# Block 2's products by token with 512 columns instead of 256, in banks that the resting attention leaves

## The chip, the cores and the metric

The kernel runs as one program on one core of a Trainium2 chip. The metric is the time of one execution on the device in microseconds (us), taken as the median over runs. Engine names as in the profile: PE is TensorE (matrix products), PEld its weight loads, DVE VectorE, ACT ScalarE, POOL GpSimd, SP SyncE (which issues DMAs).

## The reference

Two blocks over 512 tokens of width 1024, each with two layers. The change touches the second:

```python
def second_block(x, mem, ...):
    for l in range(DEPTH):                                  # 2 layers
        z = _rmsnorm(x, norm_g[l]) @ w_in[l]
        (nsa_q, nsa_kv, nsa_gate, nsa_silu, fox_qkv, fox_f, fox_silu,
         mem_q, mem_silu, merge_g) = _split(z, IN_SPLITS)
        o_a = _nsa(nsa_q, nsa_kv, ...) * silu(nsa_silu)      # 8 heads of 64, 2 key groups
        o_b = _fox(fox_qkv, fox_f, ...) * silu(fox_silu)     # 8 heads of 64, causal
        mem_kv = _rmsnorm(mem, mem_norm_g[l]) @ w_mem_kv[l]  # 256 memory rows
        o_m = _memory_xattn(mem_q, mem_kv, ...) * silu(mem_silu)   # 4 heads of 128
        g = sigmoid(merge_g).reshape(B, T, 3, D)
        u = (g[:, :, 0] * (o_a @ w_branch_a[l]) + g[:, :, 1] * (o_b @ w_branch_b[l])
             + g[:, :, 2] * (o_m @ w_branch_m[l]))
        x = x + u @ w_out[l]
```

Each attention takes a root-mean-square norm of every query and key head first; `_nsa` rotates its heads too (rope) and is the sum of three gated attentions (over compressed keys, selected blocks, a window).

## The kernel before, in words

**Arithmetic.** Every f32 operand is split into a high and a low part (`xh`, `xl` for activations, `wh`, `wl` for weights), and each product is three matmuls: high by high, high by low, low by high. A weight tile `st` comes by DMA; ACT copies `wh` out of it, and DVE (sometimes POOL) subtracts to get `wl`. In the rows below `pg<-wh,xh` is a matmul that writes bank `pg`, streams `wh` and holds `xh` as stationary weights.

**Two forms of product.** Where heads are needed token by token, `g_tm` holds 128 tokens of x and streams weights, 256 columns to a matmul; two token tiles share a bank, so the 512 tokens take two banks and 512 output columns take two passes. Where features are needed, the weights are held and 512 tokens are streamed (`pg<-xh,wh`): the merge gates (`g0`, `g1`, `g2`), the silu gates (`z0` to `z2`) and the branch outputs (`out`, `pg<-oh,wh`).

**PSUM.** Eight banks: two `pa` (scores), two `pt` (transposes), one `po` (attention values), three `pg` (products).

**Order of work.** One layer of block 2 goes through memory keys and values, memory queries, memory attention, NSA inputs, NSA attention, FoX inputs, FoX attention, the last branch's output and `w_out`. This is the foreground. The gates and branch outputs are pushed to a list of background work. Each foreground generator yields a cost, and `run` draws `cost * RATIO[i]` worth of background steps behind each yield (`pull`), the ratios standing in a table of seven:

```python
RATIO = [0.357, 0.101, 0.485, 1.137, 0.284, 0.392, 0.28]
self.pull(next(w) * r)
Fx = self.run(self.g_fox_inputs(l, pool, kp, fg), RATIO[5])
self.run(self.g_fox_attention(l, pool, Fx, zd[1], o), RATIO[6])
```

A background matmul may be put ahead of foreground work up to a distance set by `LAG`. Before `g_tm` yields `0.64 * ntok` for two slices of 128 rows of the weights, that is 20.5 us of cost for 512 columns over 512 tokens. Where a foreground waits, the background matmuls behind it fill TensorE; once the list is empty there is nothing to fill with. Four of `g1`'s tiles are held back to the end of FoX attention (`HELD`).

Of the kernel before, what the change touches and what calls it, by code (L numbers as in the profile page):

```python
# [19 lines left out]
T = 512  # L20
D = 1024
# [85 lines left out]
class Net:  # L107
# [507 lines left out]
    def rope_table(self, pool, tag, cs, g, a):  # L615

        c = self.t(pool, [128, NT, 64], tag + "c", bufs=1)
        s = self.t(pool, [128, NT, 64], tag + "s", bufs=1)
# [10 lines left out]
    def rope(self, pool, dst, src, tab, b, a):  # L629

        c, s = tab
        nh = src.shape[2]
        x, y = (
            self.t(pool, [128, 128 * nh], n).rearrange("p (t h d) -> p t h d", t=2, h=nh)
            for n in ("rpx", "rpy")
        )
        self.tt(x, src, bch(c[:, 2 * b : 2 * b + 2, :], nh, 2), ALU.mult)
        for j in range(2):
            si = src[:, j].rearrange("p h (a t f) -> p h a t f", a=a, t=2)
            yo = y[:, j].rearrange("p h (a t f) -> p h a t f", a=a, t=2)  # L640
            sj = s[:, 2 * b + j, :].rearrange("p (a t f) -> p a t f", a=a, t=2)
# [5 lines left out]
        self.tt(dst, x, y, ALU.add, self.G)  # L647

    def head_ms(self, pool, ms, src, b, h0, tag="hsq", bufs=None):

        _, _, nh, d = src.shape
        sq = self.t(pool, [128, T], tag, bufs=bufs)[:, 0 : 2 * nh * d].rearrange("p (t h d) -> p t h d", t=2, h=nh)
        self.act(sq, src, AF.Square)
        for j in range(2):
            self.V.tensor_reduce(ms[:, 2 * b + j, h0 : h0 + nh], sq[:, j], AX.X, ALU.add)
# [17 lines left out]
    def bank(self, g):  # L673

        return self.t(self.pa, [128, T], "pa") if g else self.t(self.pt, [128, T], "pt")

# [720 lines left out]
    def g_mem_inputs(self, l, pool):  # L1397
# [32 lines left out]
        def evac_k(b, ps):  # L1430
            k = ps.rearrange("p t (h d) -> p t h d", d=128)
            self.head_ms(ip, ks, k, 0, 2 * len(kr))
            a = self.t(ip, [128, D], "mt")[:, 0:T].rearrange("p (t h d) -> p t h d", t=2, h=2)
            self.act(a, k)
            kr.append(a)

        for c in range(2):
            yield from self.g_tm(w, D, 256 * c, mh, ml, evac_k, 2)
# [3 lines left out]
        for c in range(2):  # L1442
            for t in range(2):
                self.tt(kr[c][:, t], kr[c][:, t], bc(rk[:, t, 2 * c : 2 * c + 2], 128), ALU.mult)
            for i in range(2):
                kh, kl = self.t(pool, [128, T], "kh", F32R, bufs=4), self.t(pool, [128, T], "kl", F32R, bufs=4)
                self.to_fm(kh[:, 0:256], kl[:, 0:256], [kr[c][:, t, i] for t in range(2)])
                K.append((kh, kl))
        vv = []
        for c in range(2):  # L1450
            v = self.t(pool, [128, 2, 2, 256], "v", F32R)
            vh, vl = v[:, 0], v[:, 1]

            def evac_v(b, ps, vh=vh, vl=vl):
                for t in range(2):
                    self.split(vh[:, t], vl[:, t], ps[:, t], rm[:, t : t + 1])

            yield from self.g_tm(w, D, 512 + 256 * c, mh, ml, evac_v, 2)
            vv.append((vh, vl))
# [3 lines left out]
    def g_mem_query(self, l, pool):  # L1463
# [5 lines left out]
        for c in range(2):  # L1469
            qb = self.t(ip, [128, NT, 2, 128], "qb")  # L1470
            ms, r = (self.small(8, n, 2).rearrange("p (t h) -> p t h", t=NT) for n in ("qms", "qr"))

            def evac(b, ps, ms=ms, qb=qb):
                q = ps.rearrange("p t (h d) -> p t h d", d=128)
                self.head_ms(ip, ms, q, b, 0)
                for j in range(2):
                    self.tt(qb[:, 2 * b + j], q[:, j], bch(g, 2, 1), ALU.mult)

            yield from self.g_tm(I["w_in_2"][l], D, 3872 + 256 * c, self.xh, self.xl, evac)
            self.head_r(r, ms, 128, 128**-0.5, self.rt, self.rt2)  # L1480
            self.scale_heads(qb, r)
            for i in range(2):
                qh, ql = self.t(pool, [128, T], "qh", F32R, bufs=4), self.t(pool, [128, T], "ql", F32R, bufs=4)
                self.to_fm(qh, ql, [qb[:, t, i] for t in range(NT)])
                Q.append((qh, ql))
# [98 lines left out]
    def g_nsa_inputs(self, l, pool, fg):  # L1584
# [6 lines left out]
        tks = [  # L1591
            self.rope_table(rp, f"tk{b}", cs, self.row(rp, "nsa_k_norm_2", l, 64, b + 1, f"gk{b}"), 1) for b in range(2)
        ]
        kc, vc = yield from self.g_nsa_compress(l, pool, cs)
        ip, cm = self.pool(f"ni{l}", bufs=2)
        Q = []
        for c in range(2):
            qb = self.t(ip, [128, NT, 4, 64], "qb")
            msq, rq = (self.small(16, n, 2).rearrange("p (t h) -> p t h", t=NT) for n in ("msq", "rq"))

            def evac_q(b, ps, msq=msq, qb=qb):
                q = ps.rearrange("p t (h d) -> p t h d", d=64)
                self.head_ms(ip, msq, q, b, 0)
                self.rope(ip, qb[:, 2 * b : 2 * b + 2], q, tq, b, 1)

            yield from self.g_tm(w, D, 256 * c, self.xh, self.xl, evac_q)
            self.head_r(rq, msq, 64, 0.125, self.rt, self.rt2)
            self.scale_heads(qb, rq)
            for i in range(2):
                a = self.t(pool, [128, T], "qh", F32R, bufs=4), self.t(pool, [128, T], "ql", F32R, bufs=4)  # L1610
                self.to_heads(a, [qb[:, t, 2 * i : 2 * i + 2, :].rearrange("p h d -> p (h d)") for t in range(NT)])
                Q.append(a)
        K, vv = [], []
        for br in range(2):
            tk = tks[br]
            msk = self.small(8, "msk", 2).rearrange("p (t h) -> p t h", t=NT)
            rk = self.small(8, "rk", 2).rearrange("p (t h) -> p t h", t=NT)
            v = self.v_tiles(pool, 2)
            kr = []

            def evac_k(b, ps, v=v, kr=kr, msk=msk, tk=tk):
                k = ps[:, :, 0:128].rearrange("p t (h d) -> p t h d", d=64)
                self.head_ms(ip, msk, k, b, 0)
                kb = self.t(ip, [128, 2, 2, 64], "kb")
                self.rope(ip, kb, k, tk, b, 1)
                kr.append(kb)
                for j in range(2):
                    self.split_v(v, 2 * b + j, ps[:, j, 128:256])

            yield from self.g_tm(w, D, 768 + 256 * br, self.xh, self.xl, evac_k)  # L1630
            self.head_r(rk, msk, 64, 1.0, self.rt, self.rt2)
            kd = self.t(ip, [128, NT, 2, 2, 64], "qb")
            for t in range(NT):
                for u in range(2):
                    self.tt(kd[:, t, :, u, :], kr[t // 2][:, t % 2], bc(rk[:, t, :], 64), ALU.mult, self.G)
# [6 lines left out]
            vv.append(v)  # L1642
# [71 lines left out]
    def g_fox_inputs(self, l, pool, kp, fg):  # L1714
# [22 lines left out]
        Q, K, vv = [], [], []  # L1737
        for c in range(2):
            for kind in range(2):
                ms = self.small(16, "fms", 2).rearrange("p (t h) -> p t h", t=NT)  # L1740
                b4 = self.t(ip, [128, NT, 4, 64], "qb", bufs=3)

                def evac(b, ps, kind=kind, ms=ms, b4=b4):
                    q = ps.rearrange("p t (h d) -> p t h d", d=64)
                    self.head_ms(pool, ms, q, b, 0, "p", 3)
                    for j in range(2):
                        if kind == 0:
                            self.tt(b4[:, 2 * b + j], q[:, j], bch(g, 4, 1), ALU.mult)
                        else:
                            self.act(b4[:, 2 * b + j], q[:, j])  # L1750

                yield from self.g_tm(w, D, 1816 + 512 * kind + 256 * c, self.xh, self.xl, evac)
                r = self.small(16, "fr", 2).rearrange("p (t h) -> p t h", t=NT)
                self.head_r(r, ms, 64, 1.0, self.rt, self.rt2)
                if kind == 0:
                    self.scale_heads(b4, r)
                for i in range(2):
# [5 lines left out]
                    kd = self.t(ip, [128, NT, 2, 2, 64], "qb", bufs=3)  # L1763
# [8 lines left out]
            v = self.v_tiles(pool, 4)  # L1772

            def evac_v(b, ps, v=v):
                for j in range(2):
                    self.split_v(v, 2 * b + j, ps[:, j])

            yield from self.g_tm(w, D, 2840 + 256 * c, self.xh, self.xl, evac_v)
            vv.append(v)
# [179 lines left out]
```

## Time and profile before

| | |
|---|---|
| time, 3 runs | 3091.78, 3096.23, 3097.36 us; median 3096.23 |
| the profiled execution | 3096.09 us, of which the span is 3094.3 us |
| PE busy (modelled) | 3011.5 us, 97% |
| DVE, ACT, POOL busy | 2221.3 us (72%), 1502.0 us (49%), 416.4 us (13%) |
| layer 1 of block 2 | from 1773.1 to 2438.7 us of the span, 665.6 us |
| layer 2 of block 2 | from 2438.7 us to the end |

The ends of matmuls are modelled in the profile: a 512-column matmul is given 0.39 us, though the next starts sooner. So "busy" hides short waits of PE; what a matmul costs is read from one start to the next.

### The profile page before, as it was taken

What the parts mean: (1) busy time and instruction counts of PE and PEld (TensorE: products, weight loads), DVE (VectorE), ACT (ScalarE), POOL (GpSimd) and SP (SyncE); (2) the same over time, 40 slices, a digit from 0 to 9 for tenths busy, and PEclk for the clock granted to TensorE, in tenths of its full rate; (3) what the DMA queues carried; (4) which work ended last, traced back from release to release, by engine and by line L of the source; (5) the groups of instructions that cost most, each with busy time, mean ns of one, the idle gap of its engine ahead of it and who ended that gap; (6) DMA issues with size and microseconds to landing.
All of it is one profiled execution on the core that took longest, in us unless ns stands there. A gap on an engine that the chain in (4) does not pass through costs nothing. (4 is left out here: it accounts for less than half of the span.)

```text
span 3094.3 us, 54458 instructions
## 1 busy us (share of the span) xinstructions
PE 3011.5 (97%) x20148; PEld 2540.6 (82%) x20148; DVE 2221.3 (72%) x4974; ACT 1502.0 (49%) x3043; POOL 416.4 (13%) x550
## 2 busy tenths in 40 slices
PE   8989999999999899999999999999999999999999
PEld 6877778888888777788888898888888898878977
DVE  5988776777448887777774466778686666788684
ACT  3544744444324456544443344366464453476463
POOL 2433300000014343100000000200100010200200
PEclk9999999999999999999999999999999999999999
DMA  4435125333343342253333454522435545422525
GB/s 146 115 90 146 43 88 175 96 99 96 125 129 89 106 120 85 68 167 107 98 98 123 136 140 131 143 75 73 123 113 186 158 118 150 121 66 67 162 87 183
DMA packets 403116, 359.02 MB, mean 116 GB/s; under 512 B 32867, under 2 KB 350307, under 8 KB 402851
## 3 DMA queue, kind: packets, MB, share of 16 engines
q1 hardware_dynamic: 396707, 335.62, 37.6%
q0 software_dynamic: 6144, 19.93, 1.8%
q8 instruction: 159, 2.61, 0.4%
q14 instruction: 106, 0.87, 0.1%
HBM read 293.98 MB, written 61.47 MB: 115 GB/s over the span
## 5 line engine op out<-in xcount | busy, mean ns | idle before, releaser
L260 ACT ACTIVATE wh<-st 128x512 fp32r<-128x512 f32 x844 | 528.2, 629 | 788.5 <-PE pg L238 633.4
L254 DVE TENSOR_TENSOR wl<-st,wh 128x512 fp32r<-128x512 f32 x766 | 539.0, 705 | 402.0 <-ACT wh L260 397.2
L238 PE MATMUL pg<-xh,wh 128*128 128x512 f32 (+1 forms) x1824 | 733.0, 402 | 3.6 <-ACT wh L260 2.2
L238 PE MATMUL pg<-xh,wl 128*128 128x512 f32 (+1 forms) x1824 | 719.9, 395 | 5.3 <-POOL wl L254 5.3
L238 PE MATMUL pg<-xl,wh 128*128 128x512 f32 (+1 forms) x1824 | 712.2, 395 | 0.0
L238 PEld LDWEIGHTS pg<-xl,wh 128*128 128x128 f32 (+1 forms) x1824 | 343.4, 188 | 73.8 <-issue 0.4
L238 PEld LDWEIGHTS pg<-xh,wl 128*128 128x128 f32 (+1 forms) x1824 | 344.2, 189 | 72.0 <-POOL wl L254 7.0
L238 PEld LDWEIGHTS pg<-xh,wh 128*128 128x128 f32 (+1 forms) x1824 | 344.2, 189 | 70.7 <-ACT wh L260 2.6
L238 PE MATMUL pg<-wl,xh 128*128 128x256 f32 x928 | 265.1, 287 | 0.4 <-DVE wl L254 0.4
L238 PE MATMUL pg<-wh,xh 128*128 128x256 f32 x928 | 262.6, 287 | 1.1 <-DVE oz L257 0.8
L238 PE MATMUL pg<-wh,xl 128*128 128x256 f32 x928 | 263.0, 285 | 0.0
L238 PEld LDWEIGHTS pg<-wh,xh 128*128 128x128 f32 x928 | 176.3, 192 | 6.2 <-DVE oz L257 1.0
L238 PEld LDWEIGHTS pg<-wl,xh 128*128 128x128 f32 x928 | 177.9, 192 | 3.9 <-DVE wl L254 0.8
L238 PEld LDWEIGHTS pg<-wh,xl 128*128 128x128 f32 x928 | 177.7, 192 | 1.2
L485 POOL DMA_DIRECT2D xd<-xn x40 | 21.8, 544 | 1049.5 <-DVE xn L257 927.5
L254 POOL TENSOR_TENSOR wl<-st,wh 128x512 fp32r<-128x512 f32 x78 | 123.1, 1584 | 267.5 <-ACT wh L260 234.4
L238 PE MATMUL pg<-hh,wl 128*128 128x512 f32 x352 | 137.0, 389 | 0.0
L238 PE MATMUL pg<-hh,wh 128*128 128x512 f32 x352 | 136.7, 389 | 0.0
L238 PE MATMUL pg<-hl,wh 128*128 128x512 f32 x352 | 135.7, 389 | 0.0
L260 ACT ACTIVATE p<-pa,anb 128x128 f32<-128x128 f32 (+1 forms) x224 | 115.6, 517 | 36.9 <-DVE anb L725 34.0
L257 DVE SCALAR_TENSOR_TENSOR u<-pad,cols,u 128x512 f32<-128x512 f32 x176 | 127.3, 746 | 0.7
L260 ACT ACTIVATE ph<-pt 128x128 fp32r<-128x128 f32 (+1 forms) x224 | 94.9, 426 | 65.9 <-PE pt L251 64.5
(509 smaller groups left out, 6276.2 us busy)
## 6 DMA issues: line engine op xcount, KB each, us to landing
st<-in_w_in_dram SPq DMA_DIRECT2D x400, 256.0 KB
st<-in_w_up_dram SPq DMA_DIRECT2D x176, 256.0 KB
st<-in_w_down_dram SPq DMA_DIRECT2D x88, 256.0 KB
st<-in_w_out_dram SPq DMA_DIRECT2D x64, 256.0 KB
xo<-xd SPq DMA_DIRECT2D x48, 256.0 KB
th<-thz SPq DMA_DIRECT2D x48, 256.0 KB
xd<-xn POOLq DMA_DIRECT2D x40, 256.0 KB, 4.0
thd<-thz SPq DMA_DIRECT2D x32, 256.0 KB
```

The costliest lines, as they stand in the source:

```text
L238: return self.pe(self.PE.matmul(out, lhsT, rhs, start=start, stop=stop, **kw))
L254: return (eng or self.V).tensor_tensor(out, a, b, op)
L257: return self.V.scalar_tensor_tensor(out, a, s, b, op0, op1)
L260: return self.S.activation(out, in_, f, **kw)
L485: self.nc.gpsimd.dma_start(self.xd[:, k, :], x)
```

## The change

A new product `g_tmw` gives each tile of 128 tokens a bank of its own and streams 512 columns to a matmul. Three of the four banks are those of the attention, which rests meanwhile (`wide`: `pa, pa, po, pg`, or `pg, pa, pa, pg` for FoX queries, which start under the last NSA heads); memory keys and values, with two token tiles, take the two `pa`. It loads one slice of 128 rows by 512 columns at a time, as many loads and bytes as before. It yields `1.28 * len(ps)` for each slice: 41.0 of cost for 512 columns over 512 tokens.

It is used for memory keys, values and queries, NSA queries, the keys and values of NSA's two branches (together now), and FoX queries, keys and values. Compression in NSA and all of block 1 keep `g_tm`. The norms and rope are taken for one token tile with 8 heads instead of two tiles with 4, and head tiles are kept in the attention's buffers. FoX goes through all queries, all keys, all values, where before it did queries, keys and values of four heads and then of the other four. The tables `RATIO` and `LAG` stay as they are.

```diff
+    def g_tmw(self, w, K, c0, xh, xl, evac, banks):
+        ps = [self.t(p, [128, T], n) for p, n in banks]
+        nk = K // 128
+        for k in range(nk):
+            wh, wl = self.wload(w, k, 1, [(c0, 512)])
+            for t, o in enumerate(ps):
+                a, b = xh[k][:, 128 * t : 128 * t + 128], xl[k][:, 128 * t : 128 * t + 128]
+                self.mm(o, a, wh[:, 0], start=(k == 0), stop=False)
+                self.mm(o, a, wl[:, 0], start=False, stop=False)
+                self.mm(o, b, wh[:, 0], start=False, stop=(k == nk - 1))
+            if k + 1 < nk:
+                yield 1.28 * len(ps)
+        for t, o in enumerate(ps):
+            evac(t, o)
+        yield 1.28 * len(ps)
+
+    def wide(self, inner=True):
+        pa, pg = (self.pa, "pa"), (self.pg, "pg")
+        return (pa, pa, (self.po, "po"), pg) if inner else (pg, pa, pa, pg)
...
-            yield from self.g_tm(I["w_in_2"][l], D, 3872 + 256 * c, self.xh, self.xl, evac)
+        yield from self.g_tmw(I["w_in_2"][l], D, 3872, self.xh, self.xl, evac, self.wide())
...
-            yield from self.g_tm(w, D, 256 * c, self.xh, self.xl, evac_q)
+        yield from self.g_tmw(w, D, 0, self.xh, self.xl, evac_q, self.wide())
...
-            yield from self.g_tm(w, D, 768 + 256 * br, self.xh, self.xl, evac_k)
+        yield from self.g_tmw(w, D, 768, self.xh, self.xl, evac_k, self.wide())
...
-        for c in range(2):
-            for kind in range(2):
-                yield from self.g_tm(w, D, 1816 + 512 * kind + 256 * c, self.xh, self.xl, evac)
+        for kind in range(2):
+            yield from self.g_tmw(w, D, 1816 + 512 * kind, self.xh, self.xl, evac, self.wide(bool(kind)))
...
-            yield from self.g_tm(w, D, 2840 + 256 * c, self.xh, self.xl, evac_v)
+        yield from self.g_tmw(w, D, 2840, self.xh, self.xl, evac_v, self.wide())
```

TensorE has 15,542 rows in its order before and 14,136 after. The matmuls of the products that change number 1344 of 256 columns in each layer before, and 672 of 512 after. Counted in the order, for one layer (layer 2 has 10 of FoX's queries on the other side of the border between its fifth and sixth stage):

| stage (up to) | background gate matmuls | foreground product matmuls | branch-output matmuls |
|---|---|---|---|
| ahead of the first memory product | +12 | | |
| memory keys, values (first query product) | 36 → 57 | 181 → 96 | |
| memory queries (first score) | 39 → 120 | 203 → 96 | |
| memory attention (its last value product) | 132 → 51 | 96 → 86, compression's | |
| NSA inputs (first compressed score) | 128 → 99 | 384 → 202 | 96 → 96 |
| NSA attention (its last value product) | 259 → 261 | 118 → 52 | 0 → 5 |
| FoX, up to its last product | 6 → 90 | 458 → 236 | 78 → 91 |
| FoX attention, from there | 144 → 54 | | 20 → 9 |

Under NSA attention DVE makes 26 `wl`, 11 `tha` and 3 `thz` of gate work before, 20, 10 and 2 after, and two more `kl`.

Two places in TensorE's order. The first is the FoX inputs of layer 1, a slice of the weights in the last product, for the values. Before, two slices of 256 columns go to half a bank for one token tile after the other (`pg_24942` and `pg_24943` are the two banks):

```order
L238 MATMUL pg_24942<-wh_24981,xl_3547_17615 128x256
L238 MATMUL pg_24942<-wh_24981,xh_3540_17608 128x256
L238 MATMUL pg_24942<-wl_24982,xh_3540_17608 128x256
L238 MATMUL pg_24942<-wh_24981,xl_3548_17616 128x256
L238 MATMUL pg_24943<-wl_24982,xh_3539_17607 128x256
L238 MATMUL pg_24943<-wh_24981,xl_3547_17615 128x256
L238 MATMUL pg_24943<-wh_24981,xh_3540_17608 128x256
```

After, a slice of 512 columns goes to four banks (two `pa`, `po`, `pg_24201`), and nine gate matmuls into another `pg` follow it:

```order
L238 MATMUL pa_24198<-wh_24377,xl_3550_17618 128x512
L238 MATMUL pa_24199<-wh_24377,xh_3542_17610 128x512
L238 MATMUL pa_24199<-wl_24378,xh_3542_17610 128x512
L238 MATMUL pa_24199<-wh_24377,xl_3550_17618 128x512
L238 MATMUL po_24200<-wh_24377,xh_3542_17610 128x512
L238 MATMUL po_24200<-wl_24378,xh_3542_17610 128x512
L238 MATMUL po_24200<-wh_24377,xl_3550_17618 128x512
L238 MATMUL pg_24201<-wh_24377,xh_3542_17610 128x512
L238 MATMUL pg_24201<-wl_24378,xh_3542_17610 128x512
L238 MATMUL pg_24201<-wh_24377,xl_3550_17618 128x512
L238 MATMUL pg_24399<-xh_3537_17605,wh_24401 128x512
L238 MATMUL pg_24399<-xh_3537_17605,wl_24402 128x512
```

Gate work that stood behind FoX attention's heads now stands between the slices of its products. The second place is FoX attention of layer 1. Before, gate matmuls (`pg<-xh,wh`) stand between the scores (`pa`), values (`po`) and transposes (`pt`) of a head:

```order
L238 MATMUL pa_25411<-pch_23820,sel_130 128x128
L238 LDWEIGHTS identb_94
L238 MATMUL pa_25411<-neg_124,identb_94 128x128
L238 MATMUL pg_25553<-xh_3537_17605,wh_25555 128x512
L238 MATMUL pg_25553<-xh_3537_17605,wl_25556 128x512
L238 MATMUL pg_25553<-xl_3545_17613,wh_25555 128x512
L238 MATMUL po_25152<-pl_25211,v_24288 64x256
L238 MATMUL po_25152<-ph_25210,v_24288 128x256
L238 MATMUL po_25152<-pl_25211,v_24288 64x256
L238 MATMUL po_25152<-ph_25210,v_24288 128x256
```

After, from the first score to the two last heads, only attention is left:

```order
L238 MATMUL pa_24604<-pch_23343,sel_130 128x128
L238 LDWEIGHTS identb_94
L238 MATMUL pa_24604<-neg_124,identb_94 128x128
L238 MATMUL po_24502<-ph_24503,v_24196 128x256
L238 MATMUL po_24502<-pl_24504,v_24196 64x256
L238 MATMUL po_24502<-ph_24503,v_24196 128x128
L238 MATMUL po_24502<-pl_24504,v_24196 64x128
L238 MATMUL pa_24621<-kh_24106,ql_23700 128x256
L238 MATMUL pa_24621<-kl_24107,ql_23700 128x256
```

The gate product that stood in the first piece has moved ahead of the whole attention. In memory attention the same holds for eight of its sixteen tiles.

## Rows read from the trace of the kernel before

**Rows 1.** The page, part 1: busy us (share of the span) and instructions.

```profile
PE 3011.5 (97%) x20148; PEld 2540.6 (82%) x20148; DVE 2221.3 (72%) x4974; ACT 1502.0 (49%) x3043; POOL 416.4 (13%) x550
```

**Rows 2.** Busy time by stretch: the stages of layer 1 of block 2.

```profile
core 0: us, PE busy (x) PEld busy (x) DVE busy (x) ACT busy (x) POOL busy (x), PEclk, DMA share, GB/s
1773.10:1808.20 35.10, 32.88 (x239) 30.54 (x237) 25.41 (x71) 18.96 (x37) 0.00 (x0) 1.00 0.50 151
1808.20:1843.10 34.90, 34.90 (x254) 32.87 (x255) 22.68 (x63) 14.28 (x27) 2.78 (x4) 1.00 0.50 128
1843.10:1902.00 58.90, 58.90 (x372) 52.71 (x371) 40.10 (x111) 34.45 (x88) 10.28 (x15) 1.00 0.48 136
1902.00:2020.90 118.90, 117.66 (x748) 102.59 (x746) 80.11 (x225) 38.84 (x80) 22.52 (x32) 1.00 0.48 135
2020.90:2184.20 163.30, 158.40 (x1028) 134.17 (x1027) 135.33 (x417) 107.74 (x285) 3.27 (x4) 0.98 0.25 68
2184.20:2274.60 90.40, 90.40 (x646) 84.46 (x645) 60.13 (x140) 40.40 (x80) 16.74 (x39) 1.00 0.53 154
...
2349.00:2438.70 89.70, 89.70 (x406) 74.53 (x406) 57.39 (x100) 38.87 (x68) 4.36 (x8) 1.00 0.61 194
```

**Rows 3.** Busy time by stretch: FoX attention of layer 1, in pieces.

```profile
2264.30:2349.00 84.70, 80.78 (x487) 66.65 (x486) 68.77 (x161) 59.47 (x149) 1.59 (x5) 1.00 0.35 103
2288.90:2330.70 41.80, 38.39 (x250) 31.47 (x250) 37.35 (x95) 33.55 (x90) 0.00 (x0) 1.00 0.24 71
2323.40:2330.70 7.30, 5.95 (x40) 4.78 (x41) 6.39 (x17) 6.24 (x19) 0.00 (x0) 1.00 0.18 67
2330.70:2349.00 18.30, 18.30 (x97) 15.35 (x96) 10.68 (x21) 8.52 (x18) 0.00 (x0) 1.00 0.49 146
```

**Rows 4.** Timeline of PE in a run of 512-column matmuls: start us, us, instruction.

```profile
1692.81 0.39 PE L238 MATMUL pg<-hl,wh 128*128 128x512 f32 x1
...
1695.98 0.39 PE L238 MATMUL pg<-hh,wl 128*128 128x512 f32 x1
```

**Rows 5.** The same in a run of 256-column matmuls, the product for NSA's keys.

```profile
1999.70 0.28 PE L238 MATMUL pg<-wh,xh 128*128 128x256 f32 x1
...
2001.74 0.28 PE L238 MATMUL pg<-wh,xl 128*128 128x256 f32 x1
```

**Rows 6.** Groups of DVE instructions: busy us, mean ns, idle time before them.

```profile
L254 DVE TENSOR_TENSOR wl<-st,wh 128x512 fp32r<-128x512 f32 x762 | 536.7, 706 | 401.5 <-ACT wh L260 396.7 <-issue 0.2
L257 DVE SCALAR_TENSOR_TENSOR tha<-pg,R 128x512 f32<-128x512 f32 x112 | 77.0, 688 | 50.7 <-PE pg L238 35.6 <-ACT R L260 10.3 <-ACT thz L260 4.0
L730 DVE RECIPROCAL ari<-asm 128x1 f32<-128x1 f32 x288 | 45.1, 157 | 32.4 <-ACT p L260 30.5
L254 DVE TENSOR_TENSOR pl<-pt,ph 128x256 fp32r<-128x256 f32 x80 | 33.3, 419 | 18.5 <-ACT ph L260 18.2
L725 DVE TENSOR_REDUCE anb<-pa 128x1 f32<-128x256 f32 x80 | 32.8, 418 | 7.6 <-PE pa L238 6.7
L257 DVE SCALAR_TENSOR_TENSOR thz<-thz,tha 128x512 f32<-128x512 f32 x32 | 24.2, 755 | 1.1 <-ACT thz L260 0.7
L254 DVE TENSOR_TENSOR kl<-pt,kh 128x512 fp32r<-128x512 f32 x24 | 15.8, 682 | 5.0 <-ACT kh L260 5.0
L737 DVE TENSOR_SCALAR p<-p,ari 128x256 f32<-128x256 f32 x32 | 11.4, 358 | 0.6
```

**Rows 7.** Timeline of DVE in memory attention of layer 1, where a head ends.

```profile
1868.86 0.69 DVE L254 TENSOR_TENSOR oz<-po,thz 128x512 f32<-128x512 f32 x1 [2.25 <-PE po L238]
...
1870.80 0.68 DVE L254 TENSOR_TENSOR ol<-oz,oh 128x512 fp32r<-128x512 f32 x1
```

**Rows 8.** One tile over the whole program, NSA query rope: ns min/median/max.

```profile
L254 DVE TENSOR_TENSOR rpx<-pg,tqc x8: 669/681/693, 1955.4 to 2642.3; 128x512 f32<-128x512 f32 x8
```

**Rows 9.** Busy time by stretch at NSA's compressed scores of layer 1 (columns as in Rows 2).

```profile
2020.00:2025.00 5.00, 5.00 (x36) 4.79 (x34) 2.20 (x8) 1.46 (x4) 0.00 (x0) 0.78 0.37 97
2025.00:2030.00 5.00, 5.00 (x18) 4.27 (x18) 4.63 (x18) 1.76 (x5) 0.00 (x0) 0.53 0.01 2
```

More of the change, by code (lines that the diff above doesn't have):

```diff
@@ L1441, in g_mem_inputs @@
         K = []
[L1442 to L1448, printed above, removed]
+        for t in range(2):
+            self.tt(kr[t], kr[t], bc(rk[:, t], 128), ALU.mult)
+        for i in range(4):
+            kh, kl = self.t(pool, [128, T], "kh", F32R, bufs=4), self.t(pool, [128, T], "kl", F32R, bufs=4)
+            self.to_fm(kh[:, 0:256], kl[:, 0:256], [kr[t][:, i] for t in range(2)])
+            K.append((kh, kl))
         vv = []
@@ L1451, in g_mem_inputs, with evac_v @@
             v = self.t(pool, [128, 2, 2, 256], "v", F32R)
[L1452 to L1459, printed above, removed]
+            vv.append((v[:, 0], v[:, 1]))
+        def evac_v(t, ps):
+            for c in range(2):
+                self.split(vv[c][0][:, t], vv[c][1][:, t], ps[:, 256 * c : 256 * c + 256], rm[:, t : t + 1])
+        yield from self.g_tmw(w, D, 512, mh, ml, evac_v, pas)
         cm.__exit__(None, None, None)
@@ L1468, in g_mem_query, with evac @@
         Q = []
[L1469 to L1477, printed above, removed]
-            yield from self.g_tm(I["w_in_2"][l], D, 3872 + 256 * c, self.xh, self.xl, evac)
[L1480 to L1485, printed above, removed]
+        qb = self.t(ip, [128, NT, 4, 128], "qb", bufs=1)
+        ms, r = (self.t(ip, [128, NT, 4], n, bufs=1) for n in ("qms", "qr"))
+        def evac(t, ps):
+            q = ps.rearrange("p (t h d) -> p t h d", t=1, d=128)
+            self.head_ms(ip, ms, q, t, 0)
+            self.tt(qb[:, t], q[:, 0], bch(g, 4, 1), ALU.mult)
+        yield from self.g_tmw(I["w_in_2"][l], D, 3872, self.xh, self.xl, evac, self.wide())
+        self.head_r(r, ms, 128, 128**-0.5, self.rt, self.rt2)
+        self.scale_heads(qb, r)
+        for i in range(4):
+            qh, ql = self.t(pool, [128, T], "qh", F32R, bufs=4), self.t(pool, [128, T], "ql", F32R, bufs=4)
+            self.to_fm(qh, ql, [qb[:, t, i] for t in range(NT)])
+            Q.append((qh, ql))
         cm.__exit__(None, None, None)
@@ L1590, in g_nsa_inputs @@
         tq = self.rope_table(rp, "tq", cs, self.row(rp, "nsa_q_norm_2", l, 64), 1)
-        tks = [
-            self.rope_table(rp, f"tk{b}", cs, self.row(rp, "nsa_k_norm_2", l, 64, b + 1, f"gk{b}"), 1) for b in range(2)
-        ]
+        tkc, tks = (self.t(rp, [128, 2, NT, 64], n) for n in ("tkc", "tks"))
+        for b in range(2):
+            gk = self.row(rp, "nsa_k_norm_2", l, 64, b + 1, f"gk{b}")
+            self.rope_table(rp, None, cs, gk, 1, (tkc[:, b], tks[:, b]))
         kc, vc = yield from self.g_nsa_compress(l, pool, cs)
@@ L1596, in g_nsa_inputs @@
         Q = []
-        for c in range(2):
[L1598 to L1604, printed above, removed]
-            yield from self.g_tm(w, D, 256 * c, self.xh, self.xl, evac_q)
-            self.head_r(rq, msq, 64, 0.125, self.rt, self.rt2)
-            self.scale_heads(qb, rq)
+        x4 = self.heads4(pool, "ph"), self.heads4(pool, "ph")
@@ new lines, in g_nsa_inputs, with evac_q @@
+        msq, rq = (self.t(ip, [128, NT, 8], n, bufs=1) for n in ("msq", "rq"))
+        def evac_q(t, ps):
+            q = ps.rearrange("p (t h d) -> p t h d", t=1, d=64)
+            self.head_ms(ip, msq, q, t, 0)
+            self.rope(ip, [a[:, t : t + 1] for a in x4], q, tq, t, 1)
+        yield from self.g_tmw(w, D, 0, self.xh, self.xl, evac_q, self.wide())
+        self.head_r(rq, msq, 64, 0.125, self.rt, self.rt2)
+        for c in range(2):
+            self.scale_heads(x4[c], rq[:, :, 4 * c : 4 * c + 4])
@@ new lines, in g_nsa_inputs, with evac_k @@
+        K, vv, kr = [], [self.v_tiles(pool, 2) for _ in range(2)], []
+        msk, rks = (self.t(ip, [128, NT, 4], n, bufs=1) for n in ("msk", "rk"))
+        def evac_k(t, ps):
+            p3 = ps.rearrange("p (r x) -> p r x", r=2)
+            k = p3[:, :, 0:128].rearrange("p r (h d) -> p r h d", d=64)
+            sq = self.t(ip, [128, T], "hsq")[:, 0:256]
+            self.act(sq.rearrange("p (r h d) -> p r h d", r=2, h=2), k, AF.Square)
+            V.tensor_reduce(msk[:, t], sq.rearrange("p (h d) -> p h d", h=4), AX.X, ALU.add)
+            kb = self.t(ip, [128, 2, 2, 64], "kb", bufs=4)
+            self.rope(ip, kb, k, (tkc[:, :, t], tks[:, :, t]), 0, 1)
+            kr.append(kb)
+            for br in range(2):
+                self.split_v(vv[br], t, p3[:, br, 128:256])
```

112 lines of the change are left out of this document (54 added, 58 removed).

## The prediction

> **What bounds the kernel now.** I read the page first: TensorE is busy for 3011.5 of 3094.3 us [rows 1]. That share hides the point. The ends of matmuls are modelled, so I went to the busy time by stretch and, inside it, to the starts of matmuls. In layer 1 the stages with products have TensorE busy throughout, and DVE for a half to two thirds of the time (34.9 us with DVE 22.7, 90.4 with 60.1). The attention stages are different: in NSA attention DVE has 135.3 of 163.3 us and TensorE is no longer full [rows 2]. In FoX attention, five heads of 41.8 us have DVE at 37.4; the one head of them that has no gate work between its matmuls takes 7.3 us with DVE at 6.4 and ACT at 6.2 [rows 3]. So a product stage pays for each matmul that is put into it, while an attention head goes at the pace of DVE and ACT, and gate work there costs TensorE little but costs DVE its `wl` and `tha`.
>
> This is the frame for the change. Work on TensorE that is saved in a product stage is time saved. Gate work that is moved from an attention to a product is paid in full where it goes, and gives back only what the attention loses in length.
>
> **Issue.** In a run of 512-column matmuls, 14 starts lie 3.17 us apart, 0.226 us each [rows 4]; with 256 columns, 17 starts take 2.04 us, 0.120 us each [rows 5]. A pair of the latter replaced by one of the former saves 0.014 us. There are 672 such pairs in a layer, so 9.1 us, and 18.3 us over both layers. The lower bound for this is nothing (0.240 us for one matmul, if four banks in turn are as slow as two halves).
>
> The loads stay as they are in number and size (one slice of 512 columns for two of 256, and SP issues as many DMAs), and with the DMA engines at half their time in these stages [rows 2] I put the new order of loads at nothing.
>
> A rule speaks against the size of this gain. The Trainium skill, "TensorE: Matmul & The Clock Gate", section "Back-to-back issue gap", gives the isolated gap as N/2.4 + 2.5 ns. By that a pair of 256 columns takes 218 ns and one of 512 takes 216, and 1344 pairs save an estimated 3.4 us in place of 18.3. The rows differ from it (120 and 226 ns), and the measurement decides.
>
> **Where the background goes.** The yields of the changed products are twice what they were (41.0 against 20.5 for 512 columns) and the ratios are the same, so each product draws twice the gate work. I counted TensorE's order, stage by stage, and priced each at 0.226 us for a 512-column matmul. For one layer:
>
> Memory keys, values and queries: 102 gate matmuls more, +23.1 us; 384 matmuls of 256 columns become 192 of 512, −2.6. Together +20.5 on 70.0 us.
>
> Memory attention: 81 gate matmuls fewer, −18.3, and 10 of compression's 256-column ones leave, −1.2. But eight of its sixteen tiles are now without cover. DVE needs 0.418 + 0.157 + 0.419 us for each, 0.358 for every second one, whose scaling it shares with ACT [rows 6], and 0.69 + 0.68 us at the end of each of two heads [rows 7]: 12.1 us. TensorE has 12 matmuls of 256 columns and 4 transposes of 128 for two tiles, 1.7 us at the starts above, 6.7 for eight. The difference, 5.4 us, becomes visible. Together −14.1 on 58.9 us. The bounds of the 5.4 are 0 (DVE catches up under the tiles that keep cover) and 9 (each pair waits for its chain).
>
> NSA inputs: 29 gate matmuls fewer, −6.6; 384 matmuls of 256 become 192 of 512, −2.6; compression's 10 arrive, +1.2. The gate work now runs out before the keys' product, as it did before, but all eight query heads become ready at once and the next product wants the banks that they are read from. A copy-out of 512 columns by rope is 0.68 us on DVE for its first part [rows 8], and three or four such steps stand ahead of the second bank. I take +2, between 0 and +5. Together −6.0 on 118.9 us.
>
> NSA attention: the same background (259 and 261 matmuls), but DVE's share of it is smaller: six `wl`, one `tha` and one `thz` fewer, two `kl` more. That is 6 x 0.706 + 0.688 + 0.755 − 2 x 0.682 = 4.3 us by [rows 6]. Since DVE is busy for 83% of this stage [rows 2], I take −3.6, between −7 (TensorE's 118 query matmuls that become 52 count too) and +1.
>
> FoX inputs: 97 gate and branch matmuls come ahead of the end of its last product, +22.0; 458 of 256 columns become 236 of 512, −1.5.
>
> FoX attention: today the stretch from the end of the last product to the last head is 84.7 us, and the last two heads, which carry the held gate work in both kernels, take 18.3 of it [rows 3]. After, six heads without cover: 6 x 7.3 = 43.8 us. In front of them comes a start. Before, the first scores stand inside the last product. After, that product owns the score banks, so four banks must be copied out and a first tile must go through the chain. My estimate for it is 3.5 us, some five DVE instructions of 0.4 to 0.7 us. 3.5 + 43.8 + 18.3 = 65.6, −19.1. A head between 6.4 us, its DVE time, and 8.3, the mean of the five heads that are covered now, moves this by −5 to +6.
>
> Ahead of the block: 12 gate matmuls more, +2.7.
>
> The sum for a layer: +20.5 − 14.1 − 6.0 − 3.6 + 22.0 − 1.5 − 19.1 + 2.7 = +0.9; for both, +1.8 us. The profiled execution took 3096.1 us, the median is 3096.2, so the forecast is 3098 us. The 18.3 us that TensorE saves is all given back, because attention stages that have lost their filler don't get shorter by as much as the products have grown. The smaller number of norm instructions I put at nothing: they lie on DVE in product stages, where it is busy for 65%, so TensorE covers them; without that cover they would be worth 1 or 2 us.
>
> **Rivals.**
>
> *The attentions shrink further.* What speaks for it: a head's DVE time is 6.4 us and not 7.3, and with nothing else in DVE's and ACT's queues a head may come to that. Against it: the head of 7.3 us is such a head already, and both engines had 0.9 to 1.1 us of gaps in it [rows 3]. With 6.4 us for a head (−5.4 in a layer) and half of the memory tiles' 5.4 us, it is 8.1 us in a layer: 3082 us. With all lower bounds together, 3070.
>
> *The clock falls in the bare attention; the other side.* A head's columns are 3 x 1280 for scores, 2 x 1280 for values, 1280 for transposes and 512 for masks, 8192 in all: 16 times a 512-column matmul, 3.6 us at full clock. At half clock they are 7.2 us, as long as the whole head, so TensorE would become the bound there. At NSA's compressed scores, where TensorE ran short matmuls in a row, the granted clock was 0.78 and then 0.53, near the lower of its two levels, 1.2 GHz [rows 9]. Against it: in the head without gate work it was 1.00 [rows 3]. The price is between 0 and 3.6 us a head; with half, 1.8 x 12 heads = 22 us: 3120 us. [...] The Trainium skill, same page, section "HAM oscillation — how this bites in real kernels", tells of a kernel that cycles through PSUM banks, whose small idle times between groups make the clock swing. In this case's trace, products that take two banks in turn had 1.00 [rows 2]; four banks are not in it.
>
> *Four banks finish at once and the next product waits.* Six borders in a layer (memory keys to values, values to queries, NSA queries to keys, keys to attention, FoX queries to keys, keys to values) each copy out four banks with 8 heads; DVE takes some 2 us for one bank, three times 0.68 [rows 8]. Five of them exposed with 2 us each, of which 2 are in the sum already, are 8 us in a layer: 3114 us. Against it: where gate matmuls are left they stand between, and these borders have them except after NSA's queries.
>
> *It doesn't do what it says*: if a 512-column matmul into four banks in turn starts every 0.240 us, the gain of 18.3 us is gone and the rest stays: 3116 us.
>
> **How the numbers follow.** Chances: the sum as worked out 0.44, attentions shrink further 0.28, the clock 0.09, the borders 0.13, no gain from width 0.06. A measurement of this kernel can tell about 0.2% from no change, 6.2 us. The likeliest case has its own range from 3088 to 3108, and leaves the 6.2 us on either side in a fifth of its cases, 0.09 each. So faster is 0.28 + 0.09 = 0.37, slower 0.28 + 0.09 = 0.37, and within 0.2% is 0.26. The range from 3074 to 3122 takes in the rivals' times at both ends, short of all lower bounds together.
>
> **What would show each step.** Starts 0.226 us apart in the changed products, with `pa`, `pa`, `po`, `pg` in turn, show the first term. Memory keys, values and queries should be about 90 us, memory attention 45, NSA inputs 113, NSA attention 160, the stretch of FoX products up to the end of the last one 101 (80.1 before, 2184.2 to 2264.3 us [rows 2, 3]), the rest of FoX 66. Six FoX heads of 7.3 us without `wl` between them, at a clock of 1.00, show the largest term. The prediction is wrong if heads come at 6.4 or 8.3 us, if the clock in FoX attention is near 0.5, or if TensorE has gaps of 2 us or more at the borders of products.

## The result

The changed kernel is slower: 3112.73 us, median of 4 runs (3108.72 to 3116.27), against 3095.43 us for the kernel before in the same measurement. The ratio is 1.0057, with a 95% interval from 1.0045 to 1.0070. The forecast was 3098 us, in a range from 3074 to 3122. The profiled execution has a span of 3112.9 us, 18.6 us more than before.

The width itself came as forecast. The timeline of PE in the last FoX product of the changed kernel, twelve matmuls from row to row:

```profile
2287.46 0.39 PE L238 MATMUL pa<-wh,xh 128*128 128x512 f32 x1
...
2290.18 0.39 PE L238 MATMUL pg<-xh,wh 128*128 128x512 f32 x1
```

Twelve starts in 2.72 us are 0.227 us each, across the four banks `pa`, `pa`, `po`, `pg`: what a run of 512 columns showed [rows 4]. So four banks in turn cost nothing here.

The busy time by stretch, changed kernel, layer 1 (columns as in Rows 2). The borders are the first memory product, first query product, first score, last value product, first compressed score, last NSA value product, end of the last FoX product, last FoX value product:

```profile
core 0: us, PE busy (x) PEld busy (x) DVE busy (x) ACT busy (x) POOL busy (x), PEclk, DMA share, GB/s
1776.30:1813.50 37.20, 37.20 (x171) 30.24 (x170) 25.90 (x65) 19.49 (x37) 0.00 (x0) 1.00 0.62 176
1813.50:1863.90 50.40, 50.40 (x229) 41.62 (x228) 27.54 (x55) 18.54 (x33) 4.93 (x4) 1.00 0.47 126
1863.90:1904.20 40.30, 39.88 (x274) 36.04 (x273) 29.82 (x81) 26.30 (x74) 5.07 (x9) 1.00 0.41 116
1904.20:2012.80 108.60, 108.60 (x529) 86.90 (x527) 70.23 (x176) 37.65 (x78) 17.04 (x22) 1.00 0.51 144
2012.80:2189.60 176.80, 165.79 (x986) 135.72 (x985) 135.32 (x414) 108.65 (x287) 8.66 (x18) 0.95 0.24 68
2189.60:2290.10 100.50, 100.41 (x469) 83.08 (x468) 61.85 (x119) 40.39 (x71) 20.20 (x40) 1.00 0.53 159
2290.10:2360.30 70.20, 60.30 (x380) 48.10 (x379) 58.09 (x149) 51.96 (x141) 0.00 (x0) 1.00 0.22 65
```

By the same borders the kernel before took 33.1, 34.9, 57.5, 120.3, 163.2, 80.2 and 84.7 us. Against the forecast, us a layer:

| stage | forecast | layer 1 | layer 2 |
|---|---|---|---|
| memory keys, values, queries | +20.5 | +19.6 | +20.3 |
| memory attention | −14.1 | −17.2 | −17.2 |
| NSA inputs | −6.0 | −11.7 | −11.7 |
| NSA attention | −3.6 | +13.6 | +9.5 |
| FoX up to its last product | +20.5 | +20.3 | +19.5 |
| FoX attention | −19.1 | −14.5 | −14.3 |

The products grew as worked out. What the attentions gave back is where it failed, above all in NSA: inputs and attention together were to get 9.6 us shorter and got 1.9 longer in layer 1 and 2.2 shorter in layer 2. (The two have to be taken together. In layer 1 the transposes of the keys ended at 2020.8 us before, ahead of the first compressed score at 2020.9; now that score starts at 2012.8 and the keys' transposes only at 2023.9, so work of the inputs has moved over the border.) DVE is busy for 135.3 us in NSA attention, as before [rows 2], so the stage did not get more to do. It waits.

**Where NSA waits.** The timeline of DVE in the changed kernel, behind the compressed scores (in brackets the idle time ahead of an instruction, and what ended it):

```profile
2022.98 0.98 DVE L254 TENSOR_TENSOR wl<-st,wh 128x512 fp32r<-128x512 f32 x1 [2.04 <-ACT wh L260]
2027.67 0.19 DVE L254 TENSOR_TENSOR fx<-fg,r_fox_f_bias 128x32 f32<-128x32 f32 x1 [3.71 <-DMA r_fox_f_bias<-in_fox_f_bias_dram]
2027.78 0.68 DVE L254 TENSOR_TENSOR kl<-pt,kh 128x512 fp32r<-128x512 f32 x1
2028.38 0.17 DVE L1749 TENSOR_SCALAR fx<-fx 128x32 f32<-128x32 f32 x1
2028.46 0.69 DVE L254 TENSOR_TENSOR kl<-pt,kh 128x512 fp32r<-128x512 f32 x1
```

DVE stands for 3.7 us in front of a 32-column addition that belongs to FoX's gate, until the gate's bias has been loaded. Behind it in DVE's order stand the low halves of NSA's keys (`kl`). The timelines of SP and of POOL show when the bias is loaded:

```profile
2015.22 9.13 SPq L402 DMA_DIRECT2D st<-in_w_in_dram  x2
2024.96 0.34 SPq L386 DMA_DIRECT2D r_fox_f_bias<-in_fox_f_bias_dram  x1
```

```profile
2018.34 6.60 POOL L254 TENSOR_TENSOR pl<-kb,rk 128x128 f32<-128x128 f32 x16 [10.75 <-issue]
```

Its DMA stands behind two weight loads that hold SP for 9.1 us until a buffer is free. But what it waits for last is POOL, which scales the keys (`kb`) until 2024.94 us; 0.02 us later it is issued. In the kernel the bias has its buffer in the pool of FoX's inputs, which is opened when the pool of NSA's inputs, with `kb` in it, is closed; that the two share memory is read from this order and from the wait. The kernel with half yields (below) tells the two causes apart. There SP issues its last weight load at 2010.98 us, and the bias waits for POOL all the same, until 2018.61. SP's waits for it there and in the changed kernel, in this order (us in all, times, longest):

```profile
SPq L386 <- POOL pl L254: 6.3, 1, 6.3
SPq L386 <- POOL pl L254: 0.5, 1, 0.5
```

PE waits in turn:

```profile
2028.61 0.63 PE L251 MATMUL pt<-c_ident,pl 128*128 128x128 f32 x4 [2.15 <-DVE fx L1749]
```

Before, DVE waited 1.5 us for this load over both layers; now 7.4. The keys of both branches now become ready behind one product and are scaled in one run of 16, so the bias is loaded later, and the wait falls in front of the keys' low halves.

**Where FoX starts.** The timeline of PE, from the last matmul of the value product, and of DVE at the end of the first head:

```profile
2289.96 0.39 PE L238 MATMUL pg<-wh,xl 128*128 128x512 f32 x1
...
2291.54 0.22 PE L238 MATMUL pa<-kh,qh 128*128 128x128 f32 x1
...
2293.87 0.45 PE L238 MATMUL pa<-kh,qh 128*128 128x384 f32 x1 [1.33 <-ACT p L260]
```

```profile
2306.14 0.67 DVE L254 TENSOR_TENSOR ol<-oz,oh 64x512 fp32r<-64x512 f32 x1
...
2314.45 0.69 DVE L254 TENSOR_TENSOR ol<-oz,oh 64x512 fp32r<-64x512 f32 x1
...
2320.31 0.66 DVE L254 TENSOR_TENSOR ol<-oz,oh 64x512 fp32r<-64x512 f32 x1
```

From the end of the product to the end of the first head it takes 16.7 us, where the forecast had 10.8. The heads after it end 8.3 and 5.9 us apart in turn, five of them in 36.7 us, 7.3 each as forecast, at a clock of 1.00. The rest, with the last two heads, takes 16.8 us, where the forecast had 18.3.

### The profile page after: what moved, and what is told of

The parts are those of the page before. It is cut to its first block, busy times and chain, and to the rows that moved or that the text cites. A ratio compares the mean times of both kernels' runs of the same rounds, so it can differ in the third digit from the quotient of the medians.

```text
span 3112.9 us, 51600 instructions
## 1 busy us (share of the span) xinstructions
PE 3012.3 (97%) x18804; PEld 2473.7 (79%) x18804; DVE 2194.3 (70%) x4758; ACT 1497.9 (48%) x3035; POOL 415.4 (13%) x550
## 5 line engine op out<-in xcount | busy, mean ns | idle before, releaser
L238 PE MATMUL po<-ph,v 128*128 128x256 f32 x480 | 124.5, 287 | 8.5 <-ACT ph L260 8.0
L754 DVE TENSOR_REDUCE anb<-pa 128x1 f32<-128x128 f32 (+1 forms) x224 | 105.9, 475 | 25.7 <-PE pa L238 23.6
L254 DVE TENSOR_TENSOR pl<-pt,ph 128x128 fp32r<-128x128 f32 (+1 forms) x224 | 105.1, 473 | 23.5 <-ACT ph L260 22.4
L238 PE MATMUL po<-pl,v 128*64 128x256 f32 (+1 forms) x448 | 106.7, 279 | 7.6 <-DVE pl L254 7.5
L257 DVE SCALAR_TENSOR_TENSOR tha<-pg,R 128x512 f32<-128x512 f32 x112 | 76.7, 685 | 47.4 <-PE pg L238 32.6
L254 DVE TENSOR_TENSOR pad<-pg,R 128x512 f32<-128x512 f32 x112 | 77.4, 691 | 44.7 <-PE pg L238 35.9
```

Of the source, the lines that this page charges most:

```text
L238: return self.pe(self.PE.matmul(out, lhsT, rhs, start=start, stop=stop, **kw))
L254: return (eng or self.V).tensor_tensor(out, a, b, op)
L257: return self.V.scalar_tensor_tensor(out, a, s, b, op0, op1)
L754: self.V.tensor_reduce(nb, ps[:, 0:n], AX.X, ALU.max, negate=True)
```

## The experiments

The theory after the result: the width saves its 18 us; the doubled draw of gate work takes more than that away, by itself, in FoX, and by NSA's keys having nothing over them. The rival: the loss comes from the borrowed banks and from what the change does to the order of keys and heads, whatever is drawn. Times are medians; the ratio is to the kernel before on the same chip.

**Half yields.** Both yields of `g_tmw`:

```diff
-                yield 1.28 * len(ps)
+                yield 0.64 * len(ps)
...
-        yield 1.28 * len(ps)
+        yield 0.64 * len(ps)
```

> The changed kernel with half the yields in the wide product, so that a product draws as much gate work as before. By the order of instructions FoX gets its gate matmuls back (12 ahead of the end of the last product and 147 after it, as before), while memory keeps most of the shift (112 of 120 gate matmuls stay under the queries). Theory 1, the doubled draw empties FoX attention and that is the loss there: FoX comes back from 170.7 us a layer to about 163 (before 164.9, less 1.4 of issue), total about 3098. Theory 2, FoX loses because its first head cannot start inside the products any more: filled heads get longer again by what the products get shorter, FoX about 168, total about 3107.

3077.99 us, ratio 0.9941 (0.9926 to 0.9956): faster than both kernels, by 20 us more than theory 1 had for it. The stretches of layer 1 (the same borders):

```profile
1773.90:1804.70 30.80, 29.85 (x137) 23.95 (x137) 23.39 (x62) 17.80 (x33) 0.00 (x0) 1.00 0.60 175
1804.70:1853.40 48.70, 48.70 (x222) 40.15 (x221) 26.53 (x55) 18.55 (x33) 4.49 (x4) 1.00 0.50 132
1853.40:1897.80 44.40, 43.78 (x301) 40.05 (x300) 32.59 (x94) 28.02 (x79) 7.51 (x11) 1.00 0.45 123
1897.80:2010.40 112.60, 112.60 (x542) 90.41 (x541) 71.22 (x174) 39.72 (x79) 15.66 (x20) 1.00 0.50 141
2010.40:2172.60 162.20, 154.85 (x973) 126.73 (x972) 131.08 (x404) 107.57 (x285) 8.32 (x18) 1.00 0.25 70
2172.60:2250.10 77.50, 77.50 (x365) 64.41 (x364) 50.40 (x104) 33.34 (x59) 18.05 (x40) 1.00 0.53 159
2250.10:2336.60 86.50, 82.49 (x496) 67.91 (x495) 70.02 (x167) 60.48 (x155) 0.00 (x0) 1.00 0.35 102
```

FoX takes 164.0 us, near the 163 of theory 1. The rest of the difference to the changed kernel is in NSA (274.8 against 285.4) and memory (123.9 against 127.9). One thing didn't follow the draw: 112 gate matmuls still stand under the memory queries (120 in the changed kernel, 39 before). The first score wants a bank that the product holds, and the `z2` work that has to be done ahead of the attention is done here. So that shift belongs to the order and the banks, not to the yields (argued from the order, not tried by itself). FoX attention is 1.8 us longer than before, with the same gate work in it.

**The draw alone, in the kernel before.** `g_tm` gets a cost of 1.28 in the seven products:

```diff
-        yield 0.64 * ntok
+        yield cost * ntok
```

> The kernel before with the yields of the seven products doubled and nothing else: the redistribution without wide matmuls and without borrowed banks. By the sum of the prediction the emptied attentions cost what width saves, so about 3096 + 18 = 3114. If the loss comes from the borrowed banks and the late keys instead (theory 2), FoX inputs get 20 us longer and FoX attention 17 to 20 shorter, NSA and memory stay, and the total is 3096 to 3103.

3116.07 us, ratio 1.0065 (1.0050 to 1.0080), +20.6 us: the amount by which the prediction's sum has the width given back (18.3 + 1.8). Not by its stages, though: memory, NSA and FoX of layer 1 are the stretches

```profile
1773.60:1813.40 39.80, 39.80 (x270) 36.68 (x271) 28.96 (x77) 21.11 (x41) 0.00 (x0) 1.00 0.59 172
1813.40:1844.80 31.40, 31.40 (x239) 30.26 (x238) 16.26 (x45) 11.45 (x20) 2.77 (x4) 1.00 0.41 106
1844.80:1911.00 66.20, 65.44 (x395) 57.57 (x394) 44.75 (x126) 35.60 (x90) 10.15 (x15) 1.00 0.50 138
1911.00:2016.80 105.80, 104.98 (x691) 92.15 (x690) 75.02 (x219) 35.29 (x73) 18.24 (x25) 1.00 0.48 135
2016.80:2185.70 168.90, 164.87 (x1053) 139.11 (x1053) 137.03 (x421) 109.02 (x287) 5.82 (x11) 0.97 0.26 72
2185.70:2287.90 102.20, 102.20 (x698) 94.49 (x697) 63.43 (x141) 42.74 (x81) 18.44 (x40) 1.00 0.54 155
2287.90:2358.70 70.80, 61.61 (x372) 49.53 (x371) 56.42 (x141) 50.25 (x134) 0.00 (x0) 0.95 0.21 64
```

memory +11.9, NSA −8.8, FoX +8.1, where the changed kernel has +2.4, +1.9 and +5.8. So the doubled draw is a loss without wide products too, but that its total meets the prediction's sum is in part luck. In FoX the doubled draw without wide products gives nearly what the changed kernel has: inputs 22 us longer, attention 13.9 shorter. In its bare FoX attention the clock did fall, in layer 1 (0.95 in the last row above); in layer 2 it stayed at 1.00 and the stage is 1.7 us shorter:

```profile
2962.90:3032.00 69.10, 59.14 (x374) 47.32 (x374) 56.05 (x141) 50.31 (x134) 0.00 (x0) 1.00 0.17 51
```

**NSA's keys apart**, with full yields:

```diff
-        yield from self.g_tmw(w, D, 768, self.xh, self.xl, evac_k, self.wide())
+            yield from self.g_tm(w, D, 768 + 256 * br, self.xh, self.xl, evac_k)
```

> The changed kernel with the keys and values of NSA's two branches in two products of 256 columns again, as before. Theory: the keys of both branches come ready together behind one product (16 scalings on POOL in a row of 6.6 us, then transposes), so NSA's first scores are late; then NSA inputs and attention together go from 285.5 and 281.0 us to about 275 although 1.3 us of width is given up, total about 3097. Rival: the NSA time is lost in the later heads, where gate work stands in another order; then NSA stays within 3 us and the total is 3109 to 3116.

3098.79 us, ratio 1.0011 (1.0001 to 1.0020). NSA takes 276.3 and 274.7 us for 285.4 and 280.9. The last key scales are ready 9.0 us behind the last product, not 18.6. POOL is then done with the keys at 2011.4 us and the bias is loaded at once, so DVE waits 1.1 us for it over both layers, not 7.4. This run therefore doesn't tell the late keys from the late load; the next but one does.

**FoX inputs as before**, the rest changed (the whole function is the old one):

```diff
-            yield from self.g_tmw(w, D, 1816 + 512 * kind, self.xh, self.xl, evac, self.wide(bool(kind)))
+                yield from self.g_tm(w, D, 1816 + 512 * kind + 256 * c, self.xh, self.xl, evac)
```

> The changed kernel with FoX inputs as before (256 columns, four heads after four, banks of its own). It undoes the draw, the late start and the width in FoX together. FoX goes from 170.7 us a layer to the 164.9 of before, NSA and memory stay: 3101. If the later NSA heads are long because the FoX queries under them want the score banks, NSA attention gets shorter too by up to 5 us a layer: 3091.

3095.21 us, ratio 0.9997 (0.9988 to 1.0007). FoX is at 165.8 and 166.1 us, and NSA's last heads, under which FoX's queries are computed, get shorter too: the seventh 17.9 us for 20.4, from one end of `ol` to the next. So between the two expectations.

**The bias loaded early**, with full yields:

```diff
+        self.bias = self.row(pool, "fox_f_bias_2", l, 8, tag="r_fox_f_bias_2")
         rp, rcm = self.pool(f"nr{l}", bufs=1)
...
-        bias = self.row(ip, "fox_f_bias_2", l, 8)
+        bias = self.bias
```

> The changed kernel with one small load issued earlier: FoX's gate bias is loaded at the start of NSA's inputs instead of at the start of FoX's, where in the changed kernel its DMA stands on SP behind two weight loads that wait for a buffer, and DVE stands 3.7 us in each layer in front of the keys' second halves (1.5 over both layers in the kernel before). Theory, it is on the path of the first NSA scores: 3 us a layer, 3107. Rival, PE's keys are late anyhow (POOL's scalings end at the same time): within 2 us of the changed kernel, 3111 to 3114.

3104.07 us, ratio 1.0025 (1.0016 to 1.0034), 8.7 us less than the changed kernel: 4.3 a layer for one 4 KB load, for which DVE had stood 3.7 us. (The edit issues the load earlier and gives it a buffer in another pool.) NSA takes 277.2 and 277.4 us. The first head ends 151.6 us after the start of NSA's inputs for 156.4, and 151.8 for 154.9 in layer 2. With the keys apart it was 150.7 and 150.6, so most of what that run gained up to the first head is the load.

**Half yields and NSA's keys apart** (both edits above):

> Half yields and NSA's keys and values in two products of 256 columns again. Theory, the late keys are a loss of their own, whatever covers them: another 3 to 5 us a layer beside 1.3 us of width given up, 3070 against the 3078 with half yields alone. Rival, the late keys only cost where the gate work has run out, and with half yields it covers them: 3078 to 3082.

3082.61 us, ratio 0.9957 (0.9945 to 0.9970): the rival, 0.6 us above its upper end. With gate work over them the late keys cost nothing that 256 columns would save.

**Half yields and FoX inputs as before:**

> Half yields, FoX inputs as before. With half yields FoX is 164.1 us a layer and was 164.9 and 165.7 before, though width saves 1.5 us there and the queries' share under NSA. Theory, the late start of the first head eats the width: 3077 to 3081, no different from half yields alone. Rival, FoX gains by width under NSA's last heads: 3084 or more.

3084.64 us, ratio 0.9966 (0.9953 to 0.9980), 6.6 us more than half yields alone: again the rival, though the intervals of the two ratios just overlap. FoX itself is 0.9 and 1.7 us longer; the larger part is in NSA's last three heads, under which its queries are computed, 3.0 and 1.9 us.

**Half yields and the early bias:**

> Half yields and the early load of FoX's bias. DVE waits 2.6 us a layer for it with half yields. Theory, it delays the first NSA head: 3073. Rival, gate matmuls fill TensorE meanwhile and the head is bound later by DVE's whole work: within 1.5 us a layer, 3075 to 3079.

3073.60 us, ratio 0.9931 (0.9918 to 0.9945). This is the lowest median of all. It lies 4.4 us below that of half yields alone, on the theory's side, but the intervals of the two ratios overlap. In the profiled executions 3.2 of 5.0 us are in one head of layer 2 whose clock had fallen in the one and not in the other (below), and the first NSA head ends 0.7 to 0.9 us sooner in its stage. So with gate work over it the load is worth less than with full yields, about 1 us a layer by the profiles; the rest is not settled.

**Half yields in FoX alone** (`cost=0.64` in its three products):

> The changed kernel with half yields in FoX's three products alone. By the order FoX has its gate matmuls back (12 ahead, 147 after), memory and NSA inputs are as in the changed kernel, and NSA's last heads have 12 gate matmuls fewer. Theory, the draw costs where it is drawn, FoX and memory each for themselves: FoX 164 us a layer for 170.7, NSA's last two heads 4 us shorter, 3112.7 - 13 - 8 = 3092. The rest down to the 3078 of half yields everywhere is then the memory's draw, by the 24 gate matmuls a layer that NSA's late keys lack. Rival, half yields act as a whole (an earlier start of everything): 3098 or more.

3086.84 us, ratio 0.9975 (0.9965 to 0.9984), 26 us less than the changed kernel, 5 more than the theory had for it. FoX is at 164.1 us in both layers, 13.3 together; NSA at 276.8 and 279.6, with its last two heads 3.3 and 1.5 us shorter. So some three quarters of what the draw costs is drawn by FoX's products, over a third of that under NSA's last two heads, 4.8 us a layer.

**Half yields halved once more**, with the early bias:

```diff
-        yield 0.64 * len(ps)
+        yield 0.32 * len(ps)
```

> Half yields and the early bias, with the yields halved once more. By the order 10 to 20 gate matmuls a layer move from memory's products to NSA, 24 branch-output matmuls from NSA's inputs into its heads, and 57 from FoX's products to behind the last one. Theory, a gate matmul in a product is paid in full and under an attention nearly free, so less draw is better still: 3066 to 3071. Rival, the attentions are full at half yields and NSA's late keys need the cover: 3074 to 3080, no better than the 3073.6 with half yields.

3099.61 us, ratio 1.0013 (1.0004 to 1.0022), 26 us more than with half: worse than either expectation. NSA and FoX of layer 1:

```profile
1888.00:1999.50 111.50, 110.13 (x524) 86.70 (x523) 68.83 (x170) 38.06 (x78) 15.06 (x20) 1.00 0.45 130
1999.50:2174.60 175.10, 167.58 (x1013) 137.19 (x1012) 140.65 (x414) 110.53 (x289) 8.78 (x18) 0.98 0.27 78
2174.60:2241.10 66.50, 66.50 (x313) 55.25 (x312) 41.52 (x88) 29.82 (x53) 18.94 (x40) 1.00 0.37 111
2241.10:2348.30 107.20, 100.21 (x561) 81.65 (x560) 80.60 (x184) 65.33 (x162) 0.14 (x1) 0.97 0.43 131
```

The products get shorter by 11 us in FoX, and the attention longer by 20.6 (86.6 with half yields and the early bias). NSA's attention has 161.3 us with half yields and the early bias and 175.1 here, 2.9 of it in a head whose clock had fallen. Gate work under an attention is cheap only as far as the attention has gaps. In FoX two things fill them here. DVE is busy for 80.6 us, 10.5 more, and it stands for loads: branch outputs come to stand behind the products as well, and each adds to a partial sum (`ud`) that is loaded from memory. DVE's waits for it in FoX attention of layer 1, with half yields and the early bias, and here (us in all, times, longest):

```profile
DVE oz L254 <- DMA thz<-ud: 1.1, 1, 1.1
DVE oz L254 <- DMA thz<-ud: 10.9, 6, 3.0
```

How much of the loss each of the two makes is not tried by itself.

## Why the prediction came out as it did

**The range held and so did the frame; the point was 15 us low.** The frame of the prediction (a gate matmul in a product is paid in full, an attention gives back only its length) was right, and the draw alone costs 20.6 us in the kernel before, though by other stages than the sum has. The width is worth what was forecast: 0.227 us a matmul. Where it went can be read from the starts of matmuls. Each matmul's time up to the next start, summed from the first memory product of layer 1 to its last FoX value product, us:

| matmuls | before | changed | half yields |
|---|---|---|---|
| of the products (compression's among them) | 179.0 | 168.4 | 169.9 |
| of gates and branch outputs | 230.5 | 228.4 | 224.4 |
| all others: scores, values, transposes | 165.2 | 187.9 | 169.1 |

The products save 10.6 us in this layer and 10.0 in layer 2, 20.6 together for the 18.3 that were forecast. The others are the same 1311 matmuls in each kernel, and in the changed one they wait longer, by 22.7 us in layer 1 and 19.3 in layer 2. Half the yields take most of that back (3.9 us of it are left in layer 1, 4.4 in layer 2) and keep the width, so that kernel is 17.5 us faster than the one before. By an estimate from the isolated gap in the Trainium skill, "TensorE: Matmul & The Clock Gate", section "Back-to-back issue gap", 3.4 us would have been left of the width; the starts measured here decide against it.

**Issue, memory products, FoX products: right** to 1 us a layer.

**Memory attention: 3 us too dear.** The eight bare tiles were priced at 5.4 us. With 3.1 us less of it 2.3 are left, a little nearer to the bound of 0, DVE catching up under the tiles that keep cover.

**NSA inputs and NSA attention: the step that failed**, by 11.5 us in layer 1 and 7.4 in layer 2, against −9.6. It has three parts. First, the load of FoX's bias, 4.3 us a layer by its own experiment. The prediction put the new order of loads at nothing, because their number and size were unchanged and the DMA engines were half idle. It did not ask which small load now waits longer for its buffer (here until POOL has scaled the keys of both branches), and who stands behind that load's reader on DVE. Second, the last two heads are 2.5 and 1 us longer in layer 1 (2.6 and 2.1 in layer 2), where the queries of FoX draw twice as much under them; the prediction had taken 3.6 us off this stage because DVE had less of gate work, but the total of DVE's work in it (135.3 us) did not fall at all. Third, a head that took 3.1 us more in layer 1 than in layer 2, at a lower clock (below).

**FoX attention: right in kind, 4.7 us too cheap.** Bare heads came at 7.3 us. The start was sized at 3.5 us and measured 9.4 (16.7 less a head): a head's time from its first score to its end (15.3 us in the first) is longer than the distance of two heads, and the first has nobody in front of it. The estimate counted five DVE instructions and not the depth of the chain. The last two heads came 1.5 us cheaper than priced.

**The rivals.** The clock did not fall in the bare FoX attention of the changed kernel (1.00 throughout); that it can, the draw alone showed (0.95 in layer 1, where the stage took 1.7 us more than in layer 2). The kernel that cycles through PSUM banks, of which the prediction tells, stands in the Trainium skill, "TensorE: Matmul & The Clock Gate", section "A second HAM failure mode: psum-queue depth-cycling". It was not so here: products that take four banks in turn had 1.00 (FoX products, 2189.6 to 2290.1 us). Of the borders of products, the one that mattered was NSA's keys, where the gate work had run out. PE's wait of 2.15 us there is the sign that the prediction had named, and it came above all through a DMA. That doubling the yields was the thing to doubt, and not the banks, the prediction didn't say: it took the draw as given. One sum in it is off: with all its lower bounds together (5.4, 2, 3.4 and 5 us a layer) it comes to 3066 us, not 3070.

## What to carry to other kernels

When a product is made cheaper or is cut in other pieces, look at what its yields, costs or ratios draw beside it: here wide products made the kernel 17 us slower with yields that were doubled with them, and 17 us faster with half of those. Filler has an optimum: in a product it is paid in full, under an attention it is cheap up to the gaps there. With the early bias in all three, the doubled draw took 3104.07 us, half of it 3073.60 and a quarter 3099.61. After a reorder, follow each small load to what it waits for, its place in the queue and its buffer, then to the instruction that reads it and to what is queued behind that.

## What was not expected of the hardware

The granted clock in a short run of small matmuls is not decided by the order of TensorE's instructions alone. NSA's attention, with its second compressed scores of 32 columns each, is the same list of matmuls in the same order in both layers. The busy time by stretch of the changed kernel, both layers at that place:

```profile
2099.00:2103.00 4.00, 4.00 (x22) 3.90 (x22) 2.07 (x7) 0.51 (x2) 0.00 (x0) 0.55 0.00 0
2103.00:2107.00 4.00, 4.00 (x16) 3.34 (x16) 2.70 (x6) 1.59 (x5) 0.00 (x0) 0.60 0.00 0
...
2771.00:2775.00 4.00, 4.00 (x38) 3.91 (x37) 1.95 (x7) 1.83 (x5) 0.00 (x0) 1.00 0.11 33
2775.00:2779.00 4.00, 4.00 (x31) 3.64 (x30) 3.03 (x9) 1.85 (x5) 0.00 (x0) 1.00 0.02 4
```

In layer 1 the clock is near its lower level, 1.2 GHz, over these 8 us (0.55 and 0.60), and in layer 2 it stays at 2.4 GHz (1.00); that head takes 23.6 us in one and 20.5 in the other. Other kernels show about the same difference at the same place in one or both of their layers (19.5 and 22.7 us with half yields), and others in none. What decides it stays open. It may be one reason why runs of one kernel lie up to 11 us apart here.
